# The down projection of a streaming-encoder layer, recast from eight block products to seven

## The chip, the cores and the metric

The kernel runs on one core of a Trainium2 chip. The metric is the device time of one execution in microseconds (us), lower is better. The kernel before the change takes 1774.91 us (median of 3 runs, 1773.05 to 1775.65).

## What is computed

One layer of a hybrid encoder over 1056 rows (1024 of a prompt and 32 of a decoded sample), model width 1024. It has a mixing block (differential attention and retention) that ends in an addition to `h`, then a feed-forward block, then a gated addition. The part that matters here is the feed-forward block and what follows it:

```
f = rmsnorm(h, g_ffn)
g = f @ w_g;  u = f @ w_u                  # 1024 -> 2816
s = gelu(causal_dwconv3(g) + conv_b) * u
h = h + s @ w_d                            # 2816 -> 1024
h = h + (pe @ w_pe) * sigmoid(rmsnorm(h, g_pe) @ w_pg)
```

Everything is float32 in and out.

## The kernel before

Activations are held with features on the partitions and the 1056 rows along the free axis. A float32 product is made as three TensorE matmuls in a float32 format of reduced precision: each operand is split into a high part (a ScalarE copy) and a low part (a VectorE subtraction, `split_x` lines 251 to 258 and `split_w` lines 210 to 223), and `mm3` (line 242) issues high x high, high x low and low x high into one PSUM tile.

The instructions are written with a tile framework. It takes the order of the program as a priority, and each engine's queue is laid out ahead of time by a scheduler which may put a later instruction first where it reckons the earlier one not ready. An engine then works its queue strictly in that order. Buffers come from pools: a tag with `bufs=n` has n slots, and a new tile waits for a slot. Where a pool is opened on the bytes of a closed pool, its tiles wait for every user of the closed one. Nearly all loads, and the stores to the scratch tensors of this stage, are issued by SyncE's queue through `load` (line 110).

Up phase (lines 1265 to 1294). A loop over 11 blocks `b` of 256 columns makes `g` and `u` for two 128-feature tiles at a time. Each of the two products is done with seven block products instead of eight (`strassen`, line 1204, the form with fifteen additions): the rows are cut in two halves of HT = 528, the contraction in two halves, the columns in two halves of 128. Matmuls there have 264 columns (SC = HT/2). GpSimd makes the sums of weights (lines 1194 to 1200). VectorE then runs the convolution, ScalarE the gelu, GpSimd multiplies `g` by `u` (line 1293), and each finished 128 x 1056 tile of `s` goes to the scratch tensor `d_s` (line 1294). The tiles of this phase (`lx`, `ly`, `snap`, `wraw1`) lie in a pool named `late`; its `ly` tiles have six slots. The operands of the seven products lie partly in tag `A` of the pool `act` (16 slots), partly in `late`.

Down phase (lines 1323 to 1344). The 22 tiles of `s` are taken in groups of 2, 4, 4, 4, 4 and 4. A group is loaded from `d_s`, split, and multiplied by the matching rows of `w_d`, in four units `u` of 256 output columns; each unit has two 128-feature tiles `m` and three chunks of 352 rows (`fm`, line 261, PSUM tag `g` with three slots). Line 1342 adds each PSUM chunk to `hT[m]`, which is loaded from `d_h` in the first group. In the last group, `fin(m)` squares `hT[m]` (lines 969 to 975, the sum of squares on GpSimd for most m) and splits `hT[m]` times a gain for the last projection (lines 257 and 258).

End (from line 1347). `rms_rows` turns the sum of squares into a row factor `rb2`; then `w_pg` is applied to all of `f2`, eight tiles deep, and line 1358 multiplies each PSUM chunk by `rb2`.

## Time and profile before

| | |
|---|---|
| median of 3 runs | 1774.91 us |
| the profiled execution | 1772.96 us, of which the span is 1771.2 us |
| PE busy | 1747.2 us (99%) |
| VectorE (DVE) busy | 1085.8 us (61%) |
| ScalarE (ACT) busy | 722.3 us (41%) |
| GpSimd (POOL) busy | 329.7 us (19%) |
| up phase, roughly | 950 to 1403 us of the span |
| down phase, roughly | 1399 to 1662 us |

PE is TensorE's matmul stream, PEld its weight loads, SP is SyncE (SPq its queue of transfers). Matmuls are pipelined, so the duration of one is longer than the distance from one to the next; how many fall in a stretch is the better measure. `L1342` is line 1342 of the kernel. `out<-in` names what an instruction writes and reads.

### The profile page before, as it was taken

Reading aid. Unit: us, or ns where it says so; the run is one execution under the profiler, and the core shown is the slowest. Engines: PE = TensorE matmul, PEld = TensorE weight load, DVE = VectorE, ACT = ScalarE, POOL = GpSimd, SP = SyncE. Lnnn points to the kernel's source line nnn. Section 1 sums busy time; section 2 is a strip of 40 time slices with the busy share of each in tenths; the row PEclk is TensorE's granted clock in tenths of the full one; section 3 lists DMA queues with packets and bytes.
Section 4 is the critical chain, followed back from the end, with each engine's and each line's share of the span. In section 5 each row is a group of like instructions: output and inputs, shape, how many; then the busy total and the mean of one; then the engine's idle time right before and its main releaser. Section 6 shows DMA issues by size and latency. Waiting matters only on the chain.

```text
span 1771.2 us, 31680 instructions
## 1 busy us (share of the span) xinstructions
PE 1747.2 (99%) x12626; PEld 1719.7 (97%) x12626; DVE 1085.8 (61%) x2352; ACT 722.3 (41%) x1623; POOL 329.7 (19%) x356
## 2 busy tenths in 40 slices
PE   7999999999999999999999999999999999999998
PEld 7998999999999999999999999999999999999998
DVE  7766766666664564565468866665566664444644
ACT  6536664656423433322346433443333421112332
POOL 6110001000121021000002433344443200001111
PEclk9999999999999999999999999999999999999999
DMA  9311222222222214544443222222222552211331
GB/s 289 107 49 41 72 73 76 83 67 78 71 79 65 74 63 142 205 146 138 159 161 125 85 83 86 73 73 73 73 85 90 203 208 97 73 38 47 110 110 50
DMA packets 136858, 178.12 MB, mean 101 GB/s; under 512 B 9645, under 2 KB 115973, under 8 KB 136709
## 3 DMA queue, kind: packets, MB, share of 16 engines
q1 hardware_dynamic: 119976, 145.53, 25.5%
q0 software_dynamic: 8896, 26.06, 4.2%
q10 hardware_dynamic: 7837, 4.51, 0.9%
q8 instruction: 99, 1.62, 0.4%
q14 instruction: 50, 0.41, 0.1%
HBM read 128.92 MB, written 47.14 MB: 99 GB/s over the span
## 4 chain that ended last, share of the span: by engine, by line
PE 91%; DVE 4%; DMA 3%; ACT 1%; issue 1%; SPq 0%; ACTq 0%; DVEq 0%
PE gt L247 19%; PE gt L248 19%; PE gt L249 19%; PE gt L1220 4%; PE gt L1221 4%; PE gt L1219 4%; PE st L1220 2%; PE st L1221 2%; PE st L1219 2%; PE mt L659 2%; PE mt L1219 1%; PE mt L1220 1%; PE mt L1221 1%; PE st L622 1%; PE st L623 1%; PE gt L478 1%
## 5 line engine op out<-in xcount | busy, mean ns | idle before, releaser
L247 PE MATMUL gt<-apair,whi 128*128 128x352 f32 x672 | 219.5, 327 | 0.1
L248 PE MATMUL gt<-apair,whi 128*128 128x352 f32 x672 | 219.1, 326 | 0.0
L249 PE MATMUL gt<-apair,wlo 128*128 128x352 f32 x672 | 218.4, 326 | 0.0
L1179 DVE TENSOR_TENSOR wlo<-wraw,whi 128x512 fp32r<-128x512 f32 x154 | 140.2, 918 | 102.7 <-ACT whi L1178 101.8
L220 ACT ACTIVATE whi<-wraw 128x512 fp32r<-128x512 f32 x196 | 119.2, 629 | 203.0 <-PE gt L248 174.4
L247 PE MATMUL gt<-sA,whi 128*128 128x352 f32 x528 | 170.3, 323 | 1.3 <-DVE lx L1342 1.3
L248 PE MATMUL gt<-sA,whi 128*128 128x352 f32 x528 | 170.3, 322 | 0.0
L249 PE MATMUL gt<-sA,wlo 128*128 128x352 f32 x528 | 170.3, 322 | 0.0
L1178 ACT ACTIVATE whi<-wraw 128x512 fp32r<-128x512 f32 x154 | 96.8, 632 | 171.8 <-PE st L1220 69.0
L221 DVE TENSOR_TENSOR wlo<-wraw,whi 128x512 fp32r<-128x512 f32 x196 | 135.2, 706 | 27.9 <-ACT whi L220 25.0
L1221 PE MATMUL gt<-opt,wlo 128*128 128x264 f32 x528 | 150.5, 285 | 1.2 <-DVE wlo L1179 1.2
L1220 PE MATMUL gt<-opt,whi 128*128 128x264 f32 x528 | 150.4, 285 | 0.0
L1219 PE MATMUL gt<-opt,whi 128*128 128x264 f32 x528 | 149.8, 284 | 0.5 <-ACT whi L1178 0.5
L247 PE MATMUL gt<-whi,apair 128*128 128x256 f32 x512 | 147.4, 289 | 0.4 <-DVE apair L378 0.4
L248 PE MATMUL gt<-wlo,apair 128*128 128x256 f32 x512 | 146.9, 287 | 0.0
L249 PE MATMUL gt<-whi,apair 128*128 128x256 f32 x512 | 146.3, 286 | 0.0
L1342 DVE TENSOR_TENSOR lx<-lx,gt 128x352 f32<-128x352 f32 x144 | 73.6, 517 | 92.6 <-PE gt L249 92.5
L249 PEld LDWEIGHTS gt<-apair,wlo 128*128 128x128 f32 x672 | 126.3, 188 | 1.9 <-issue 0.2
L247 PEld LDWEIGHTS gt<-apair,whi 128*128 128x128 f32 x672 | 126.4, 188 | 1.7 <-DVE etile L781 0.3
L248 PEld LDWEIGHTS gt<-apair,whi 128*128 128x128 f32 x672 | 126.5, 188 | 1.4
L247 PEld LDWEIGHTS gt<-sA,whi 128*128 128x128 f32 x528 | 99.1, 188 | 2.0 <-DVE lx L1342 1.9
L1221 PEld LDWEIGHTS gt<-opt,wlo 128*128 128x128 f32 x528 | 99.2, 188 | 1.4 <-DVE wlo L1179 1.4
(419 smaller groups left out, 4991.0 us busy)
## 6 DMA issues: line engine op xcount, KB each, us to landing
wraw<-in_w_in SPq DMA_DIRECT2D x28, 512.0 KB, 4.0
d_s<-ly SPq DMA_DIRECT2D x22, 528.0 KB, 2.7
wraw<-in_w_g SPq DMA_DIRECT2D x22, 512.0 KB, 5.1
wraw<-in_w_u SPq DMA_DIRECT2D x22, 512.0 KB, 3.8
wraw<-in_w_d SPq DMA_DIRECT2D x20, 512.0 KB, 3.6
d_gt<-etile POOLq DMA_DIRECT2D x48, 176.0 KB, 2.1
ly<-d_gt SPq DMA_DIRECT2D x16, 528.0 KB, 3.7
ly<-d_s SPq DMA_DIRECT2D x16, 528.0 KB, 4.7
```

The source lines that it names most:

```text
L220: S.activation(hi, r, AF.Copy)
L221: V.tensor_tensor(out=lo, in0=r, in1=hi.bitcast(F32), op=ALU.subtract)
L247: PE.matmul(ps, wh, xh, start=first and i == 0, stop=False)
L248: PE.matmul(ps, wh, xl, start=False, stop=False)
L249: PE.matmul(ps, wl, xh, start=False, stop=last and i == n - 1)
L659: PE.matmul(po, pt[:, i * 128:i * 128 + 128], v[:, b + i, :], start=b + i == 0, stop=b + i == t)
L1178: S.activation(h3, src, AF.Copy)
L1179: V.tensor_tensor(out=l3, in0=src, in1=h3.bitcast(F32), op=ALU.subtract)
L1219: PE.matmul(ps, wh[:, ws], xh, start=start and k == 0, stop=False, skip_group_check=True)
L1220: PE.matmul(ps, wh[:, ws], xl, start=False, stop=False, skip_group_check=True)
L1221: PE.matmul(ps, wl[:, ws], xh, start=False, stop=k == n - 1, skip_group_check=True)
L1342: V.tensor_tensor(out=hT[m][:, c0:c0 + n], in0=hT[m][:, c0:c0 + n], in1=ps, op=ALU.add)
```

## The change

The down projection is recast in the same seven-product form. The contraction of 2816 is cut in two halves by the parity of the 128-feature tile (j = 0 or 1, 11 tiles each), the rows in two halves of 528, and each unit of 256 output columns in two halves of 128. For each of the seven products in turn, over all four units, 11 tiles deep, two chunks of 264 rows are accumulated in PSUM and then added to the halves of `hT` that need them. The seven row operands (four quarters and their sums) are made by VectorE at the end of each block of the up phase and go to a new scratch tensor `d_q` instead of `d_s` (NB = 11 below). Sums of weights are made by GpSimd. The pool `late` is closed after the up phase, and a pool `down` is opened on its bytes, with a pool `sums` inside that is closed ahead of the seventh product and replaced by a pool `last`.

```
+    d_q = dram.tile([7 * NB * 128, HT], F32, name="d_q")
...
+    lps = ctx.enter_context(ExitStack())
+    lp = pool("late", stack=lps)
...
+    QROWS = ("b11", "t2", "b21", "b22", "t3", "t1", "t4")
...
                 G.tensor_tensor(out=ss[j][:, a:e], in0=ss[j][:, a:e], in1=ys[j][:, a + o:e + o], op=ALU.mult)
-            load(d_s[ft * 128:(ft + 1) * 128, :], ss[j])
+        (b11_, b12_), (b21_, b22_), (t3_, t1_) = ((x[:, 0:HT], x[:, HT:T]) for x in (ss[0], ss[1], ys[0]))
+        t4_ = ys[1][:, 0:HT]
+        V.tensor_tensor(out=t3_, in0=b22_, in1=b12_, op=ALU.subtract)
+        V.tensor_tensor(out=t1_, in0=b11_, in1=b12_, op=ALU.subtract)
+        V.tensor_tensor(out=b12_, in0=t3_, in1=b11_, op=ALU.add)
+        V.tensor_tensor(out=t4_, in0=b12_, in1=b21_, op=ALU.subtract)
+        for n, x in ((0, ss[0]), (2, ss[1]), (4, ys[0])):
+            load(q_rows(n, 2, b), x[:, 0:T].rearrange("p (n c) -> p n c", n=2))
+        load(q_rows(6, 1, b), t4_.unsqueeze(1))
...
+    lps.close()
+    PRODUCTS = ("b21", "b11", "t1", "t2", "t3", "b22", "t4")
+    dn = pool("down")
+    hT = [dn.tile([128, T], F32, name="hT", tag="H", bufs=KD) for _ in range(KD)]
+    for m in range(KD):
+        load(hT[m], d_h[m * 128:(m + 1) * 128, :])
...
+    def stage(n, b):
+        nm = PRODUCTS[n]
+        q = QROWS.index(nm)
+        if n == 0:
+            if b % 2 == 0:
+                c = min(2, NB - b)
+                staged = ap_.tile([128, 2, HT], F32, name="stg", tag="A", bufs=16)
+                load(staged[:, 0:c, :], q_rows(q, 1, b, c))
...
+            return
+        raw = dn.tile([128, HT], F32, name="stg", tag="T", bufs=3)
+        load(raw, q_rows(q, 1, b)[:, 0, :])
+        split_row(n, b, raw)
...
+    def raw_w(i, j, u, own=None, wide=None):
+        src = wv[j][:, :, u * 256 + i * 128:u * 256 + i * 128 + 128]
+        nraw[0] += 1
+        if wide is None:
+            wide = nraw[0] % 2
+        if own is None and not wide:
+            ta, tb = (wp.tile([128, 1024], F32, name="wraw", tag="raw", bufs=2) for _ in range(2))
+            load(ta.rearrange("p (k c) -> p k c", c=128), src[:, 0:8, :])
+            load(tb[:, 0:384].rearrange("p (k c) -> p k c", c=128), src[:, 8:NB, :])
+            return [ta[:, 0:512], ta[:, 512:1024], tb[:, 0:384]]
+        t = own if own is not None else dn.tile([128, NB * 128], F32, name="wr", tag="W", bufs=1)
+        load(t.rearrange("p (k c) -> p k c", c=128), src)
+        return [t[:, 0:512], t[:, 512:1024], t[:, 1024:1408]]
...
+        elif nm == "t1":
+            t = sb.tile([128, NB * 128], F32, name="wsum", tag="B", bufs=4)
+            w = wsum[u] = add_w(raw_w(1, 0, u, own=t), raw_w(1, 1, u, wide=u % 2))
+        elif nm == "t2":
+            w = add_w(wsum[u], raw_w(0, 0, u))
+        elif nm == "b22":
+            w = add_w(wsum[u], raw_w(0, 1, u))
+        else:
+            w = add_w(raw_w(0, 0, u, wide=u % 2), raw_w(1, 0, u, wide=1 - u % 2))
...
+    for n, nm in enumerate(PRODUCTS):
+        if n == 6:
+            sbs.close()
+            lp, ybufs = pool("last"), 5
         for u in range(4):
...
+            ws = product_w(n, u)
+            he, ho = hT[2 * u], hT[2 * u + 1]
+            for c0 in (0, SC):
+                ps = gt(SC)
+                mm3(ps, ws, [(xo[n, k][:, 0, c0:c0 + SC], xo[n, k][:, 1, c0:c0 + SC]) for k in range(NB)])
+                a, b_ = slice(c0, c0 + SC), slice(HT + c0, HT + c0 + SC)
+                if nm == "b21":
+                    acc_into(he[:, a], ps)
+                elif nm == "b11":
+                    copy(rr[u][:, a], ps)
+                    acc_into(he[:, a], ps)
+                elif nm == "t1":
+                    acc_into(he[:, b_], ps)
+                    acc_into(ho[:, b_], ps, ALU.subtract)
+                elif nm in ("t2", "t3"):
+                    acc_into(rr[u][:, a], ps)
+                elif nm == "b22":
+                    acc_into(he[:, b_], ps)
+                else:
+                    acc_into(ho[:, a], ps, ALU.subtract)
+            if nm == "t2":
+                acc_into(he[:, HT:T], rr[u])
+            elif nm == "t3":
+                acc_into(ho[:, HT:T], rr[u], ALU.subtract)
+                acc_into(ho[:, 0:HT], rr[u], ALU.subtract)
+            if n < 6:
+                for b in range(3 * u, min(3 * u + 3, NB)):
+                    stage(n + 1, b)
+            else:
+                for m in ((0, 2), (4, 6), (1, 3), (5, 7))[u] if u < 3 else ():
                     fin(m)
+    fin(5)
+    fin(7)
```

`split_row` splits a staged row operand into a tile of tag `A`, or of a new tag `Q` (six slots in `down`) for the first six tiles of every second product. `acc_into` is one VectorE addition or subtraction, `add_w` three GpSimd additions (128 x 512, 512 and 384). `rr` holds running sums in 128 x 528 pieces.

## Rows read from the trace of the kernel before

**Rows 1.** The page: span and busy time of each engine, and the chain that ended last, by engine.

```profile
span 1771.2 us, 31680 instructions
...
PE 1747.2 (99%) x12626; PEld 1719.7 (97%) x12626; DVE 1085.8 (61%) x2352; ACT 722.3 (41%) x1623; POOL 329.7 (19%) x356
...
PE 91%; DVE 4%; DMA 3%; ACT 1%; issue 1%; SPq 0%; ACTq 0%; DVEq 0%
```

**Rows 2.** Windows of the span: start:end and length, then busy time (and instructions) of PE, PEld, DVE, ACT and POOL, granted TensorE clock, DMA share and GB/s. Two windows of the up phase, the change of phase, two windows of the down phase.

```profile
1100.00:1200.00 100.00, 100.00 (x822) 100.00 (x821) 63.03 (x111) 40.88 (x80) 37.73 (x30) 1.00 0.23 75
1200.00:1300.00 100.00, 100.00 (x823) 100.00 (x822) 58.30 (x105) 38.40 (x77) 42.26 (x31) 1.00 0.27 86
...
1400.00:1450.00 50.00, 48.71 (x313) 48.00 (x312) 34.59 (x57) 14.35 (x21) 6.68 (x6) 1.00 0.83 304
1450.00:1500.00 50.00, 50.00 (x315) 50.00 (x314) 23.36 (x40) 10.11 (x14) 0.00 (x0) 1.00 0.26 86
1500.00:1550.00 50.00, 50.00 (x314) 50.00 (x313) 23.39 (x40) 8.85 (x12) 0.00 (x0) 1.00 0.24 75
```

**Rows 3.** What PE waited for from 1380 us to the end: us in total, times, longest.

```profile
PE gt L247 <- DVE lx L1342: 1.3, 2, 1.0
PE mt L1370 <- ACT mtile L134: 0.8, 1, 0.8
```

**Rows 4.** Instructions by line and shape, 1410 to 1650 us (the down phase): busy us, mean ns of one, idle before.

```profile
L1342 DVE TENSOR_TENSOR lx<-lx,gt 128x352 f32<-128x352 f32 x135 | 69.1, 518 | 92.6 <-PE gt L249 92.5
L221 DVE TENSOR_TENSOR wlo<-wraw,whi 128x512 fp32r<-128x512 f32 x44 | 31.5, 721 | 12.9 <-ACT whi L220 12.9
L220 ACT ACTIVATE whi<-wraw 128x512 fp32r<-128x512 f32 x44 | 27.5, 629 | 139.8 <-PE gt L248 119.4 <-DMA wraw<-in_w_d 13.7 <-issue 5.1
L255 DVE TENSOR_TENSOR sA<-ly,sA 128x1056 fp32r<-128x1056 f32 x16 | 19.9, 1251 | 2.8 <-ACT sA L254 2.8
...
L975 POOL TENSOR_TENSOR ly<-ly 128x1056 f32<-128x1056 f32 x4 | 9.9, 2470 | 227.8 <-ACT ly L974 227.8
```

**Rows 5.** The same for 1100 to 1300 us (the up phase): the multiplication on GpSimd, one of its additions of weights, an addition from PSUM.

```profile
L1293 POOL TENSOR_TENSOR ly<-ly 128x1024 f32<-128x1024 f32 x10 | 24.9, 2512 | 7.3 <-ACT ly L1257 7.3
...
L1194 POOL TENSOR_TENSOR wraw<-wraw,wraw 128x512 f32<-128x512 f32 x10 | 12.9, 1286 | 114.9 <-DVE wlo L1179 114.9
L1262 DVE TENSOR_TENSOR ly<-mt,snap 128x264 f32<-128x264 f32 x20 | 8.1, 422 | 0.0
```

**Rows 6.** Transfers. From the page: SyncE's queue over the whole span (packets, MB, share of 16 engines), the store of a tile of `s` and a load of weights (KB each, median us to landing). From the window 381 to 388 us, in which nearly all packets of the queue are of 512 bytes: the queue. From the window 1405 to 1425 us: GB/s in 40 slices, and the queue.

```profile
q1 hardware_dynamic: 119976, 145.53, 25.5%
...
d_s<-ly SPq DMA_DIRECT2D x22, 528.0 KB, 2.7
...
wraw<-in_w_d SPq DMA_DIRECT2D x20, 512.0 KB, 3.6
...
q1 hardware_dynamic: 1080, 0.54, 26.7%
...
GB/s 359 291 259 358 374 389 414 422 422 397 378 383 384 410 417 412 422 414 406 438 414 406 397 422 414 422 366 385 355 387 367 442 418 406 414 422 397 389 367 379
...
q1 hardware_dynamic: 3354, 7.82, 102.3%
```

**Rows 7.** The earlier change of pools, from `p1` to `late`: what SyncE's queue waited for from 690 to 701 us; the last VectorE instruction that reads a tile of `p1` (`ft`); the first loads into `late` (start, us).

```profile
SPq L110 <- DVE mtile L867: 13.8, 1, 13.8
...
699.10 0.25 DVE L867 SCALAR_TENSOR_TENSOR mtile<-mt,gda,ft 128x32 f32<-128x32 f32 x1 [1.73 <-PE mt L865]
...
699.50 0.81 SPq L110 DMA_DIRECT2D ly<-d_od  x2
```

**Rows 8.** The end of the up phase in order of time (start us, us): two VectorE instructions, three multiplications on GpSimd, and the loads of `hT`.

```profile
1398.15 1.82 SPq L110 DMA_DIRECT2D lx<-d_h  x4
...
1405.21 5.40 POOL L1293 TENSOR_TENSOR ly<-ly 128x1024 f32<-128x1024 f32 x3 [2.39 <-ACT ly L1257]
...
1407.00 0.49 DVE L1262 TENSOR_TENSOR ly<-st,snap 128x232 f32<-128x232 f32 x2 [3.29 <-PE st L1221]
...
1408.29 2.22 DVE L221 TENSOR_TENSOR wlo<-wraw,whi 128x512 fp32r<-128x512 f32 x1 [0.36 <-ACT whi L220]
```

**Rows 9.** The end of the down phase in order of time: one addition of squares on GpSimd, the split of `hT` beside it and one without company, the last addition from PSUM, and the two instructions by which `rb2` reaches the first chunk of the last projection.

```profile
1640.08 2.46 POOL L975 TENSOR_TENSOR ly<-ly 128x1056 f32<-128x1056 f32 x1 [3.84 <-ACT ly L974]
...
1641.03 2.62 DVE L258 SCALAR_TENSOR_TENSOR f<-lx,cvec,f 128x1056 fp32r<-128x1056 f32 x1 [1.00 <-ACT f L257]
...
1659.88 1.31 DVE L258 SCALAR_TENSOR_TENSOR f<-lx,cvec,f 128x1056 fp32r<-128x1056 f32 x1
...
1662.47 0.52 DVE L1342 TENSOR_TENSOR lx<-lx,gt 128x352 f32<-128x352 f32 x1
...
1675.08 0.69 DVE L1000 COPY ly<-mt 128x512 f32<-128x512 f32 x1 [4.21 <-PE mt L995]
1675.80 0.52 DVE L1358 TENSOR_TENSOR etile<-gt,ly 128x352 f32<-128x352 f32 x1
```

**Rows 10.** The first 30 us in three windows, columns as in rows 2.

```profile
0.00:10.00 10.00, 3.02 (x10) 1.90 (x10) 4.07 (x26) 5.30 (x11) 2.83 (x9) 1.00 0.82 244
10.00:20.00 10.00, 7.04 (x41) 6.65 (x41) 6.84 (x18) 2.77 (x8) 3.60 (x5) 1.00 1.03 367
20.00:30.00 10.00, 9.67 (x67) 9.28 (x67) 9.40 (x41) 8.43 (x21) 8.31 (x13) 0.83 1.07 317
```

More of the change, by code (lines that the diff above doesn't have):

```diff
@@ L908, in layer_kernel @@
         gate_unit(6)
-    lp = pool("late")
+    lps = ctx.enter_context(ExitStack())
+    lp = pool("late", stack=lps)
+    ybufs = 6
     def xtile(dt=F32):
@@ L916, in ytile @@
     def ytile(n=T, dt=F32):
-        return lp.tile([128, n], dt, name="ly", tag="Y", bufs=6, padded_shape=[128, 1060])
+        return lp.tile([128, n], dt, name="ly", tag="Y", bufs=ybufs, padded_shape=[128, 1060])
     def snap():
@@ L1301, in layer_kernel @@
     store(O["conv_sample"].rearrange("o b w (f p) -> (o b w f) p", p=128), ct[44:88, 0:128])
-    hT = [None] * KD
-    f2 = []
+    lps.close()
[4 more added lines that the diff above has]
+        load(hT[m], d_h[m * 128:(m + 1) * 128, :])
+    r2 = (rstd_b, dn.tile([128, T], F32, name="r2", tag="R", bufs=1))
+    rr = [r2[u // 2][:, u % 2 * HT:u % 2 * HT + HT] for u in range(4)]
+    sbs = ctx.enter_context(ExitStack())
+    sb = pool("sums", stack=sbs)
+    wsum = [None] * 4
+    wv = I["w_d"][0].rearrange("(b j p) c -> j p b c", j=2, p=128)
+    f2 = [None] * KD
     acc2 = [None]
@@ L1310, in f2_tile @@
         nx[0] += 1
[L1311 to L1312 removed]
+        if nx[0] <= 6:
+            return dn.tile([128, T], F32R, name="f2q", tag="Q", bufs=6)
+        if nx[0] == 7:
+            return dn.tile([128, T], F32R, name="f2r", tag="R", bufs=1)
         return ap_.tile([128, T], F32R, name="f2", tag="A", bufs=16)
@@ L1320, in fin @@
             split_x(fp[0][:, cs], fp[1][:, cs], hT[m][:, cs], gpe[:, m:m + 1])
[L1321 to L1343 removed]
+        f2[m] = fp
@@ new lines, in split_row @@
+    def split_row(n, b, raw):
+        if n % 2 and b < 6:
+            t = dn.tile([128, 2, HT], F32R, name="oq", tag="Q", bufs=6)
+        else:
+            t = ap_.tile([128, 2, HT], F32R, name="oq", tag="A", bufs=16)
+        split_x(t[:, 0, :], t[:, 1, :], raw, -1.0 if PRODUCTS[n] == "t2" else None)
+        xo[n, b] = t
+    nraw = [1]
+    def raw_w(i, j, u, own=None, wide=None):
[11 more added lines that the diff above has]
+        return [t[:, 0:512], t[:, 512:1024], t[:, 1024:1408]]
@@ new lines, in add_w, with product_w @@
+    def add_w(dst, src):
+        for x, y in zip(dst, src):
+            G.tensor_tensor(out=x, in0=x, in1=y, op=ALU.add)
+        return dst
+    def product_w(n, u):
+        nm = PRODUCTS[n]
+        if nm == "b21":
+            w = raw_w(0, 1, u)
+        elif nm == "b11":
+            w = raw_w(0, 0, u)
+        elif nm == "t4":
+            w = raw_w(1, 1, u)
+        elif nm == "t1":
[7 more added lines that the diff above has]
+            w = add_w(raw_w(0, 0, u, wide=u % 2), raw_w(1, 0, u, wide=1 - u % 2))
+        parts = []
+        for x in w:
+            c = x.shape[1]
+            hi = wp.tile([128, 512], F32R, name="whi", tag="hi", bufs=6)
+            lo = wp.tile([128, 512], F32R, name="wlo", tag="lo", bufs=6)
+            split_x(hi[:, :c], lo[:, :c], x)
+            parts.append((hi, lo))
+        return [tuple(y[:, k % 4 * 128:k % 4 * 128 + 128] for y in parts[k // 4]) for k in range(NB)]
@@ new lines, in acc_into @@
+    def acc_into(dst, src, op=ALU.add):
+        V.tensor_tensor(out=dst, in0=dst, in1=src, op=op)
+    for b in range(NB):
+        stage(0, b)
+    for b in range(NB):
+        split_row(0, b, xo.pop(("raw", b)))
+    for n, nm in enumerate(PRODUCTS):
+        if n == 6:
+            sbs.close()
+            lp, ybufs = pool("last"), 5
+        for u in range(4):
+            ws = product_w(n, u)
[4 more added lines that the diff above has]
+                a, b_ = slice(c0, c0 + SC), slice(HT + c0, HT + c0 + SC)
+                if nm == "b21":
+                    acc_into(he[:, a], ps)
+                elif nm == "b11":
+                    copy(rr[u][:, a], ps)
[17 more added lines that the diff above has]
+                    stage(n + 1, b)
+            else:
+                for m in ((0, 2), (4, 6), (1, 3), (5, 7))[u] if u < 3 else ():
```

30 lines of the change are left out of this document (6 added, 24 removed).

## The prediction

> **What bounds the kernel now.** I read the page first: PE is busy 99% of the span and carries 91% of the chain that ended last [rows 1]. Then the windows: in the up phase and in the down phase PE is busy every microsecond at full clock, while DVE, ACT, POOL and the DMA engines have room; only the change between the two phases shows a gap, 1.3 us of 50 [rows 2]. Then the waits of PE: 1.3 us for VectorE at that change and 0.8 us later, nothing else [rows 3]. So the stage pays for matmuls by number and width, and whatever the change adds costs time only where it makes PE wait. The work is to count matmuls, then to look for places where the new form leaves PE without operands, weights or PSUM.
>
> **Term 1, the matmuls.** Before: 22 tiles x 8 m x 3 chunks x 3 passes = 1584 matmuls of 352 columns. 315 and 314 of them fall in two windows of 50 us [rows 2], so one takes 0.1590 us and all take 251.8 us. After: 7 products x 4 units x 2 chunks x 11 tiles x 3 passes = 1848 of 264 columns. The up phase issues just these, 822 and 823 in 100 us [rows 2]: 0.1216 us each, 224.7 us. An eighth less arithmetic therefore gives back only 10.8% of the time, since the narrower matmul costs more per column: **-27.1 us**. A unit (66 matmuls) lasts 8.03 us, a chunk 4.01.
>
> **Term 2, the change of phase.** All tiles of `down` wait for every user of `late`. The earlier change of pools shows it: SyncE sat 13.8 us, and its first loads left 0.15 us after the last reader of an old tile had ended [rows 7]. There PE had other units to run; here little is left. Call the end of the last up matmul T0.
> - What can run: the first product's row operands lie in `act`, outside the closed pool, and its rows (b21) come from `ss[1]`, stored early; the weights of unit 0 use the old `raw` slots, and after them those of unit 2. Unit 1's weights go to tag `W` in `down`. With three PSUM slots and no `hT` to add into, PE can run unit 0 and half of unit 2, to T0 + 12.
> - When the pool opens: the last additions from PSUM (0.8 us after the matmul, as 1407.00 + 0.49 [rows 8]), the product of `g` and `u` for one tile on POOL (2.51 us, and 0.5 for its 32 last columns [rows 5]), the four new VectorE instructions of 528 elements (half of 1251 ns [rows 4], some 0.65 us each, 2.6), then the last stores: 2.7 us for one alone [rows 6], and some 1.2 us more since three are under way, 1.35 MB in all. T0 + 10.3.
> - What then stands in SyncE's queue, by program order: eight loads of `hT` (4.33 MB, 11 us at the 390 GB/s of the saturated queue [rows 6]), three row tiles of the second product (0.8 MB, 2.1 us), and only then unit 1's weights: 1408 packets of 512 bytes. The window with such packets alone gives 0.267 x 7 us x 16 / 1080 = 27.7 ns each [rows 6], so 2.4 us over 16 engines. With some 2 us from issue to first bytes (3.6 us of landing for a load that needs 1.4 us) and 1.6 us of splitting (0.63 on ACT, 0.7 on DVE [rows 4], 0.3 between them): T0 + 29.4.
> - `hT[0]` lands at T0 + 13.7, which frees PSUM for the other half of unit 2. PE thus has 16.06 us of work in 29.4: it stands some 13.3 us, less the 1.3 us of today [rows 2]: **+12**. That the scheduler puts unit 2 ahead of unit 1 I take from the loads of `hT` that today run 4 to 9 us ahead of the last up-phase work on POOL and DVE [rows 8]: the queues don't keep program order where something is late. Bounds: 3.4 (weights ahead of `hT`) and 20.1 (no reordering), both worked out under the rivals.
>
> **Term 3, the clock.** After ten microseconds with PE busy 3.02 and ten with 7.04, the granted clock of the next ten was 0.83 although PE was busy 9.67 of them [rows 10]: 1.7 us at full speed were lost. The gap of term 2 is of that kind; today's 1.3 us left the clock at 1.00 [rows 2]. **+1.7**, bounds 0 and 3.4 (two such falls).
>
> **Term 4, the up phase.** Each block (41 us) gets four VectorE instructions, 2.6 us, on an engine that is 58 to 63% busy there, and four transfers for two, on DMA engines 0.23 to 0.27 busy [rows 2]. The cover is PE's own queue of matmuls; six `ly` slots still meet six tiles a block, held some 4 us longer, and the next block needs its third to sixth tile only half a block later. **+1**; bounds 0 and 29 (11 x 2.6, every instruction on the path), the value being near the end that today's gapless windows suggest.
>
> **Term 5, inside the seven products.** What DVE needs per unit: three splits of weights (0.69 + 0.69 + 0.53 = 1.9), 2.75 splits of row tiles (1.8), two additions from PSUM at 0.42 [rows 4, 5], two more in `t1`, one addition of 528 (0.65) in `t2`, two in `t3`. So 4.6 us in `b21`, `b11`, `b22` and `t4` (ahead of `fin`), 5.4 in `t1`, 5.2 in `t2`, 5.9 in `t3`, out of 8.03. POOL adds weights in four products: 1.29 + 1.29 + 0.97 = 3.55 us a unit [rows 5]. But the two don't run freely side by side: a weight split that takes 0.72 us took 2.22 beside the multiplications of POOL, and ended with them, at 1410.5 [rows 8]; a split of `hT` took 2.62 us beside POOL and 1.31 alone [rows 9]. An addition from PSUM kept its 0.52 us throughout [rows 4, 9]. So I add POOL's time to that of the DVE instructions with two SBUF inputs: `t1` 7.25, `t2` 7.9, `t3` 8.55, `b22` 7.25, and count half of the PSUM additions behind them: 8.1, 8.3, 9.0, 7.7 us, four units each, 132 against PE's 128.5. Weights are split up to two units ahead (six slots, three a unit) and the light second product gives room, so part of the 3.8 us is absorbed: **+2**, bounds 0 and 12. Transfers: in `t3` a unit moves 2816 packets (4.9 us) and 0.8 MB of rows (2.0), 6.9 of 8.03; its weight loop (4.5 us to land, 3.6 adding, 1.3 splitting, 9.4) is longer than a unit, but over four units it falls behind by 4 us of the 8 it leads.
>
> The Trainium skill, "SBUF — State Buffer", section "Who interferes with whom", says that a VectorE instruction with two SBUF inputs and a GpSimd instruction that reads SBUF share an exclusive port, the later one waiting for the whole of the other. The rows above agree for VectorE; that POOL waits as well no row shows. It speaks against this change, and becomes the first rival.
>
> **Term 6, the tail.** The eight `fin` had four units of 11.4 us; now they have 32 us. In SBUF instructions: 8 splits at 1.31, weights 4 x 1.9 and 2.8 for `w_pg`, five additions of squares on POOL at 2.47 and 2.8 us on DVE [rows 4, 9] make 36 us against PE's 32.1. Half of these can start early, since even m are complete one product before. Today `rb2` is in use 13.3 us after the last addition from PSUM [rows 9] and PE just covers it (three chunks of 24 matmuls, 11.5 us, and the transposes), so lateness counts in full: **+3**, bounds -1 and +8.
>
> **The sum.** -27.1 + 12 + 1.7 + 1 + 2 + 3 = -7.4 us on an execution of 1772.96 (span 1771.2 and 1.76 around it): 1765.6. The median of the runs lies 1.95 us above that execution: **1767.5 us**, 0.4% faster. A change of this kernel can be told from none by about 0.2%, 3.5 us.
>
> **The rivals.**
> - *The shared port of DVE and POOL sets the pace of `t1` to `b22` and of `fin`.* If PSUM additions don't fit beside POOL, a unit takes 8.94, 8.75, 9.4 and 8.1 us: 12.3 us over PE, and the tail 8. It decides once a unit's sum exceeds 8.03 us for more units than the two of lead. -27.1 + 12 + 1.7 + 1 + 12.3 + 8 = +7.9: 1782.8, slower. For it: instructions that ended with POOL's. Against: today's up phase has both engines busy and no wait of PE [rows 2]. 0.17.
> - *PE keeps the written order of units.* It stands from T0 + 8.03 to 29.4, 21.4 us, less 1.3: term 2 is 20.1, and the result 1775.6, no change. Against: [rows 8]. 0.16.
> - *Unit 1's weights go ahead of `hT`.* They land at T0 + 14.7, `hT[0]` at 16.1; its addition frees PSUM at 16.7, so PE stands 4.7 us after its 12.0 of work, term 2 is 3.4, and the fall of the clock costs 0.8 less: 1758.1. For it: SyncE's queue is laid out by need, too. 0.20.
> - *Small packets throttle the stage.* 50,688 of 512 bytes at 60 ns, the mean over all packets of this queue (0.255 x 1771.2 us x 16 / 119976 [rows 6]), would be 190 us of all 16 engines, and 20.8 MB of rows 53 more: 243 against 224.7, +18 over the terms less the gap: about 1783. Against: the 27.7 ns of packets of this size. 0.05.
> - The forecast: 0.42.
>
> **How the numbers follow.** Faster by over 0.2% (below 1771.4): four fifths of the forecast, all of the third rival, a fifth of the second: 0.57. Within 0.2%: the rest of the forecast, most of the second rival, a little of the first: 0.19. Slower: 0.24. The range 1754 to 1784 reaches from the third rival, with terms 5 and 6 at their low ends, to the first with its full price; the forecast's own range is 1760 to 1776.
>
> **What would show it.** 1848 matmuls of 264 columns at 0.1216 us; a gap of 10 to 16 us in PE within 30 us of the last up matmul, ended by a split of weights loaded to tag `W`, and a granted clock below 1.00 in that stretch; SyncE waiting for the last user of `late`; in `t3`, PE waiting for weights or PSUM for under 5 us; PE waiting for `rb2` by about 3 us at the start of the last projection. Wrong would be: no gap at the change of phase, waits of over 10 us spread over `t1` to `b22`, or a gap in the up phase.

## The result and the profile after

The kernel after takes 1796.48 us (median, 1794.56 to 1800.66) where the kernel before takes 1774.07 beside it: a ratio of 1.0129, 95% interval 1.0106 to 1.0151. It is 1.3% slower; the prediction was 1767.5 us, and its range ended at 1784.

The page of the kernel after, the lines that answer to [rows 1]:

```profile
span 1796.5 us, 32815 instructions
...
PE 1733.9 (97%) x12890; PEld 1703.5 (95%) x12890; DVE 1144.1 (64%) x2423; ACT 767.0 (43%) x1726; POOL 399.6 (22%) x404
...
PE 10%; DMA 5%; DVE 2%; POOL 1%; SPq 1%; issue 1%; ACT 1%; DVEq 0%; POOLq 0%; ACTq 0%
```

PE is busy 13 us less, yet the span is 25.3 us longer. The chain that ended last now carries transfers, VectorE and GpSimd beside PE (its shares add up to some 21% because it reaches back only to 1415.7 us, where the down phase begins): the stage is no longer bound by matmuls alone. The windows (columns as in [rows 2]) show where:

```profile
1100.00:1200.00 100.00, 100.00 (x822) 100.00 (x821) 67.31 (x121) 40.63 (x79) 37.55 (x29) 1.00 0.28 92
...
1410.00:1420.00 10.00, 7.35 (x46) 7.35 (x47) 9.35 (x15) 1.62 (x3) 0.62 (x2) 0.67 0.54 186
1420.00:1430.00 10.00, 2.44 (x21) 2.23 (x19) 0.80 (x3) 0.00 (x0) 0.00 (x0) 0.84 1.00 398
1430.00:1440.00 10.00, 2.99 (x13) 2.99 (x14) 4.96 (x9) 4.73 (x9) 0.00 (x0) 0.50 1.06 319
...
1500.00:1550.00 50.00, 43.28 (x336) 43.07 (x336) 32.20 (x44) 14.03 (x26) 26.95 (x19) 0.93 0.61 173
1550.00:1600.00 50.00, 47.43 (x383) 46.60 (x382) 34.66 (x54) 20.06 (x34) 9.65 (x7) 1.00 0.61 179
1600.00:1650.00 50.00, 42.46 (x315) 41.63 (x316) 35.78 (x44) 20.53 (x34) 24.65 (x17) 0.93 0.48 137
```

The up phase is as gapless as before. At the change of phase PE does 12.8 us of work in 30, and at a lower clock; then it loses again and again, most where POOL is busy. What PE waited for, from 1395 to 1690 us in three stretches (us in total, times, longest):

```profile
PE gt L248 <- ACT whi L255: 14.6, 1, 14.6
PE gt L249 <- DVE oq L256: 5.6, 1, 5.6
...
PE gt L248 <- DVE hT L1432: 8.5, 2, 6.7
...
PE gt L250 <- DVE wlo L256: 2.7, 2, 2.1
PE gt L248 <- DVE rstd_b L1432: 2.4, 2, 1.3
```

(`whi` and `wlo` are split weights, `oq` split rows, `hT` and `rstd_b` additions that free PSUM.) One measure serves all that follows: the **loss** of a unit is the distance from its first matmul to that of the next unit, less 8.03 us. Undisturbed units last 8.03 to 8.06 us, as predicted. The loss of the 28 units is 52.6 us: 41.6 in 15 gaps of over 0.3 us, 10.5 in 106 matmuls at half clock (0.22 us apart for 0.12), the rest small (the profiled execution took 1798.3 us, 1.8 above the median). By product, in the order in which they run, in us: b21 24.0, b11 3.8, t1 9.4, t2 3.0, t3 3.1, b22 9.3, t4 0.0. The last up matmul starts within 0.2 us of where it did before, so the account is: from it to the last addition of the phase 277.9 us, where before it was 255.8 (1662.47 [rows 9] less 1406.68), +22.1; behind that +3.4.

**The two waits at the change of phase**, in order of time (start us, us): VectorE, then SyncE's queue, then the two splits of weights on ACT.

```profile
1410.65 0.71 DVE L1308 TENSOR_TENSOR ly<-ly 128x528 f32<-128x528 f32 x1 [3.31 <-POOL ly L1304]
...
1411.90 1.32 DVE L256 TENSOR_TENSOR oq<-stg,oq 128x528 fp32r<-128x528 f32 x2
...
1412.01 4.67 SPq L111 DMA_DIRECT2D d_q<-ly  x3
1418.64 4.04 SPq L111 DMA_DIRECT2D hT<-d_h  x8
1422.73 2.51 SPq L111 DMA_DIRECT2D stg<-d_q  x3
1426.22 0.38 SPq L111 DMA_DIRECT2D wr<-in_w_d  x1
...
1436.33 1.56 ACT L255 ACTIVATE whi<-wr 128x512 fp32r<-128x512 f32 x3 [2.14 <-DMA wr<-in_w_d]
1437.80 1.55 ACT L255 ACTIVATE whi<-wraw 128x512 fp32r<-128x512 f32 x3
```

The 5.6 us lie inside unit 0: the low splits of its row tiles stand on VectorE behind the last block's row sums, and the first of these waits for POOL's multiplication. The 14.6 us follow the predicted order: the pool opens 12.1 us after the last up matmul (1406.5), `hT` goes first, the rows of b11, then unit 1's weights into tag `W`, split from 1436.3 on. But on ACT the weights of unit 2 (`wraw`, loaded into old slots before) are split behind them, as written, so PE could run no matmul of unit 2 in between.

**One of the later waits**, the 6.7 us that end at 1513.64, in the same columns:

```profile
1500.91 4.73 POOL L1402 TENSOR_TENSOR wsum<-wsum,wraw 128x512 f32<-128x512 f32 x3
...
1504.38 1.66 SPq L111 DMA_DIRECT2D wraw<-in_w_d  x2
1506.09 1.43 SPq L111 DMA_DIRECT2D stg<-d_q  x3
...
1511.86 0.64 ACT L258 ACTIVATE oq<-stg 128x528 fp32r<-128x528 f32 x1 [10.34 <-DMA stg<-d_q]
...
1512.53 0.71 DVE L259 SCALAR_TENSOR_TENSOR oq<-stg,oq 128x528 fp32r<-128x528 f32 x1 [7.76 <-ACT oq L258]
1513.16 0.42 DVE L1432 TENSOR_TENSOR hT<-hT,gt 128x264 f32<-128x264 f32 x1
```

Read it from the end. PE's next chunk needs the PSUM slot that the addition at 1513.16 frees. Its operand was there when PE's wait began, but it stands on VectorE behind a row split; the split waits for ACT, ACT for a row tile's load; the load stands on SyncE behind two weight loads, and these wait for slots that POOL's additions of weights free. Five queues, each in order, none of them full.

### The profile page after: what moved, and what is told of

It is laid out like the page before. It is cut to its first block, busy times and chain, and to the rows that moved or that the text cites. A ratio compares the mean times of both kernels' runs of the same rounds, so it can differ in the third digit from the quotient of the medians.

```text
span 1796.5 us, 32815 instructions
## 1 busy us (share of the span) xinstructions
PE 1733.9 (97%) x12890; PEld 1703.5 (95%) x12890; DVE 1144.1 (64%) x2423; ACT 767.0 (43%) x1726; POOL 399.6 (22%) x404
## 5 line engine op out<-in xcount | busy, mean ns | idle before, releaser
L248 PE MATMUL gt<-oq,whi 128*128 128x264 f32 x616 | 180.2, 293 | 30.4 <-ACT whi L255 16.2
L1183 DVE TENSOR_TENSOR wlo<-wraw,whi 128x512 fp32r<-128x512 f32 x154 | 140.0, 917 | 82.5 <-ACT whi L1182 81.5
L249 PE MATMUL gt<-oq,whi 128*128 128x264 f32 x616 | 180.2, 293 | 5.6 <-DVE oq L256 5.6
L250 PE MATMUL gt<-oq,wlo 128*128 128x264 f32 x616 | 180.1, 293 | 2.8 <-DVE wlo L256 2.7
L1182 ACT ACTIVATE whi<-wraw 128x512 fp32r<-128x512 f32 x154 | 96.8, 632 | 171.8 <-PE st L1224 68.0
L248 PEld LDWEIGHTS gt<-oq,whi 128*128 128x128 f32 x616 | 121.0, 197 | 32.2 <-ACT whi L255 18.0
L249 PEld LDWEIGHTS gt<-oq,whi 128*128 128x128 f32 x616 | 120.7, 196 | 5.8 <-DVE oq L256 5.8
L250 PEld LDWEIGHTS gt<-oq,wlo 128*128 128x128 f32 x616 | 120.8, 196 | 3.4 <-DVE wlo L256 3.4
L221 ACT ACTIVATE whi<-wraw 128x512 fp32r<-128x512 f32 x152 | 91.8, 629 | 63.9 <-PE gt L249 56.8
L222 DVE TENSOR_TENSOR wlo<-wraw,whi 128x512 fp32r<-128x512 f32 x152 | 103.9, 702 | 15.8 <-ACT whi L221 12.2
```

Source lines behind the costliest of these rows:

```text
L221: S.activation(hi, r, AF.Copy)
L222: V.tensor_tensor(out=lo, in0=r, in1=hi.bitcast(F32), op=ALU.subtract)
L248: PE.matmul(ps, wh, xh, start=first and i == 0, stop=False)
L249: PE.matmul(ps, wh, xl, start=False, stop=False)
L250: PE.matmul(ps, wl, xh, start=False, stop=last and i == n - 1)
L1182: S.activation(h3, src, AF.Copy)
```

## The experiments

Losses in us, by the measure above. The kernel before took 1773.4 to 1774.1 beside them throughout. e1 to e10 are one execution each, and the four of the kernel after lie between 1794.6 and 1800.7, so times a few us apart are not told apart by one execution; the losses come from one profiled execution. In e1, e4, e7, e8 and e11 to e15 the first matmul of the phase starts 1.36 us after the last up matmul, for 0.12 in the kernel after; these 1.24 us the table leaves out.

```
kernel                 median us   b21   b11  t1 to t4
after                    1796.48  24.0   3.8   24.8
e1_first_weights         1789.43  17.8   6.3   19.8
e4_first_psum            1789.88  17.1   6.4   21.5
e2_no_weight_sums        1785.43  24.2   2.3   13.9
e9_sums_on_dve           1786.67  24.7   5.4   12.8
e5_rows_no_load          1790.38  26.5   0.0   18.5
e6_rows_act_queue        1788.26  25.7   1.7   16.8
e10_no_sums_no_loads     1771.72  27.5   0.0    0.0
e3_rows_once             1766.21  22.2   0.0    0.0
e8_sums_later            1784.31  12.1   3.9   22.3
e7_change_of_phase       1783.97   8.6   3.7   26.8
e11_ordered              1783.26   7.3  11.7   21.3
e12_ordered_dve          1778.18   7.1  19.9    9.2
e13_two_queues           1770.15  14.2   2.2    9.4
e14_less_at_once         1767.31   8.5   5.2    8.4
e15_splits_first         1765.76   5.6   4.0   10.2
```

Against the expectations below: e8, e9, e10 and e13 came out as one of their theories had it, to within a microsecond. e2 and e5 came out as their rivals had it, with 14 and 18 us still lost from t1 on, and e3 lost nothing there. Outside what any of their theories had put lie e1 (7 us gained, for 15 to 19 or under 6), e6 (16.8 us left, for under 12) and e12 (9.2 us left, for under 8, and 1778 us for 1757 to 1768). e4 stayed with e1 instead of falling to 1774 to 1779, and e7 and e11 lost 12.3 and 19.0 us in the first two products where under 7 and 8 were expected, as their rivals had it. e14 and e15 are taken up at their place.

### The gap: e1 and e4

e1 loads all weights of the first product into the old slots, which are open early.

```
-            w = raw_w(0, 1, u)
+            w = raw_w(0, 1, u, wide=0)
```

> The changed kernel, with all four units of the first product loading their weights into the old raw slots, none into the tag W of the pool that opens late. Theory A (the gap of 14.6 us after unit 0 is unit 1's weights, which stand behind the close of the old pool and eight loads of hT, while PE keeps the written order): the gap shrinks to the wait for hT[0], under 4 us, and the clock falls once less, so 15 to 19 us less than the changed kernel's 1796. Rival (hT itself is what is late; weights are only the last to arrive): the gap stays over 10 us, ended by an addition into hT, and the time changes by less than 6 us. Neither expects a change in the waits of the later products, some 20 us.

The 14.6 us went, but the time fell by 7 only. The waits of PE from 1395 to 1490 us:

```profile
PE gt L249 <- DVE oq L256: 5.1, 1, 5.1
PE gt L248 <- ACT whi L255: 3.7, 1, 3.7
PE gt L248 <- issue: 2.8, 1, 2.8
PE gt L248 <- ACT oq L255: 1.7, 2, 1.1
PE gt L248 <- DVE hT L1432: 1.7, 1, 1.7
```

The wait for rows stayed (5.1); the one of 14.6 has become five shorter ones: on weights, on rows, on PSUM and, in one ("issue"), on nothing that the profile names. e4 adds more PSUM slots for the first product:

```
-                ps = gt(SC)
+                ps = (gt, gt, st, st, mt, mt, gt, st)[2 * u + (c0 > 0)](SC) if n == 0 else gt(SC)
```

> The edit of e1, and the first product's eight chunks in PSUM tiles of all three tags, so that no matmul of it waits for an addition into hT. Theory A: only the wait for the last block's row tile (5.6 us at 1412 in the changed kernel) is left of the 20 us, 1774 to 1779; if hT paces e1, e4 is faster than e1 by what e1's gap still shows, otherwise the two are within 2 us.

No gain: PSUM waiting for `hT` isn't what limits that stretch.

### From b11 on: sums of weights, row loads, or both (e2, e9, e5, e6, e10, e3)

e2 leaves the additions of weights out and keeps their loads.

```
-        for x, y in zip(dst, src):
-            G.tensor_tensor(out=x, in0=x, in1=y, op=ALU.add)
         return dst
```

> The changed kernel with GpSimd's additions of weights left out: the products t1, t2, t3 and b22 multiply by one of their loaded weights instead of the sum; all loads stay. Theory B (the additions pace the weight slots, SyncE's in-order queue waits there with the row loads behind, and the PSUM additions wait behind the row splits): the excess of 24 us in the units of t1 to b22 over 8.03 us each falls below 6 us, time 1772 to 1780. Rival B1 (the row tiles, by their loads and splits alone, are late whatever POOL does): at least 12 us of the excess stay, time above 1784. Both leave the 20 us at the change of phase.

e9 makes the same sums on VectorE.

```
-            G.tensor_tensor(out=x, in0=x, in1=y, op=ALU.add)
+            V.tensor_tensor(out=x, in0=x, in1=y, op=ALU.add)
```

> The changed kernel with the 48 additions of weights on VectorE in place of GpSimd. Theory D (in t1 to b22 the additions on POOL and the row and weight splits on DVE hold each other up at a shared port, so each unit pays POOL's 3.55 us on DVE's side; on DVE the same additions take some 1.9 us and nothing waits for a port): the excess of 24 us after the first product falls to 8 to 18 us, what late row loads alone leave (16 us in e2), time 1782 to 1791. Rival D1 (DVE is simply full, port or not): 1.9 us more a unit on DVE makes it worse, above 1798.

e5 leaves the row loads out from b11 on: one tile that stays in place is split each time.

```
-        load(raw, q_rows(q, 1, b)[:, 0, :])
-        split_row(n, b, raw)
+        split_row(n, b, ident_row)
```

> The changed kernel with the 66 later row tiles split as before, but all from one tile that is loaded once: the loads of row tiles are left out, the splits on ACT and DVE and all weights and sums stay. Theory C (row loads arrive late, because they stand in SyncE's in-order queue behind weight loads that wait for a slot, and PSUM additions stand on DVE behind the splits of the late rows): the waits after the first product vanish to under 4 us, as they did in e3, and the time is 1765 to 1771. Rival C1 (the engine time of the splits beside POOL, the shared port): 10 us or more of the 24 us stay, 1776 or above.

e6 keeps the loads, and issues them from ScalarE's queue.

```
-        load(raw, q_rows(q, 1, b)[:, 0, :])
+        S.dma_start(out=raw, in_=q_rows(q, 1, b)[:, 0, :])
```

> The changed kernel with the 66 later loads of row tiles issued by ScalarE's queue instead of SyncE's. Theory C: rows no longer stand behind weight loads, so the excess of 24 us in the later products falls below 12 us, time 1779 to 1787. If the transfers themselves are the limit (bytes and packets), nothing changes: 1793 to 1799. If ScalarE's queue takes over the blocking, since it waits for a row slot that DVE frees, waits for splits of weights grow and the time may exceed 1796.

e10 has the edits of e2 and e5 together; e3 takes the first product's row operands for all seven, with neither loads nor splits of rows, and keeps the sums.

```
-                    stage(n + 1, b)
+                    xo[n + 1, b] = xo[0, b]
```

> The edits of e2 and e5 together: no additions of weights and no loads of the 66 later row tiles; all splits and all weight loads stay. Theory E (two separate causes, the additions beside the splits and the late row loads; the splits alone fit): no wait is left after the first product, as in e3, time 1766 to 1771 (with the gap of the change of phase at 18 to 23 us). Rival E1 (the splits alone overfill DVE or ACT): 5 us or more stay, above 1773.

> The changed kernel with the row operands of the first product used for all seven: the 66 later row tiles are neither loaded nor split; the additions of weights stay. Theory B (the weight loop and POOL are too slow, rows only pass the delay on to the PSUM additions): with no row split ahead of a PSUM addition most waits for hT go, but waits for weights in t1, t3 and b22 stay: 4 to 12 us of the 24 us remain, time 1775 to 1788. Rival B1 (rows alone): all of it goes and the later products run without a wait, time near 1771. Rival B2 (the port shared by VectorE and POOL sets the pace): DVE loses 1.8 us a unit, and the waits for weights go as well.

Four of these make a square. Loss from b11 to t4: both 28.6, no sums 16.2, no row loads 18.5, neither 0.0. Either cause alone costs 16 to 18 us, taking only one away gives back 10 to 12, and without both the splits, the additions from PSUM and 1848 matmuls fit exactly. e6 gives as much as having no row loads at all (18.5): what hurt was their place in SyncE's queue behind weight loads, not their bytes. e9 gives nearly as much as having no sums (18.2 against 16.2), though VectorE then does more: what hurt was their being on POOL beside VectorE, not the sums. The instructions by line and shape, 1450 to 1690 us (busy us, mean ns of one, idle before), in the kernel after:

```profile
L256 DVE TENSOR_TENSOR oq<-stg,oq 128x528 fp32r<-128x528 f32 x50 | 40.2, 827 | 36.7 <-ACT oq L255 36.5
L256 DVE TENSOR_TENSOR wlo<-wsum,whi 128x512 fp32r<-128x512 f32 x24 | 25.6, 1092 | 3.7 <-ACT whi L255 3.7
...
L1402 POOL TENSOR_TENSOR wsum<-wsum,wr 128x512 f32<-128x512 f32 x12 | 17.8, 1502 | 10.2 <-DMA wr<-in_w_d 7.4 <-DVE wlo L256 2.7
```

and in e9:

```profile
L256 DVE TENSOR_TENSOR oq<-stg,oq 128x528 fp32r<-128x528 f32 x50 | 34.3, 706 | 21.4 <-ACT oq L255 21.2
L256 DVE TENSOR_TENSOR wlo<-wsum,whi 128x512 fp32r<-128x512 f32 x24 | 16.0, 685 | 0.2 <-ACT whi L255 0.2
...
L1402 DVE TENSOR_TENSOR wsum<-wsum,wr 128x512 f32<-128x512 f32 x12 | 7.8, 687 | 10.7 <-DMA wr<-in_w_d 10.7
```

A weight split takes 1092 ns beside POOL and 685 without; POOL's addition takes 1502 ns here and 1286 in the up phase [rows 5]. Both engines lose. VectorE does the same addition in 687 ns, in less than half of POOL's time, so e9 alone doesn't separate a slow POOL from the two engines holding each other up.

e3 helps to separate them: it is without row work and loses nothing from b11 on, although its sums are still on POOL and hardly faster there, as its row for the same instruction shows.

```profile
L1402 POOL TENSOR_TENSOR wsum<-wsum,wr 128x512 f32<-128x512 f32 x12 | 16.9, 1429 | 8.5 <-DMA wr<-in_w_d 8.5
```

POOL's own pace is therefore enough, and e5, which differs from e3 by the row splits alone, loses 18.5 us. That fits a VectorE which, with the row splits gone, has room for the stretched rest.

### The change of phase: e8, e7, e11, e12

e8 is e1 with t1's own weight loads, 2.9 MB that stood in the first 40 us, held behind b11's last row load (`after` fixes an order of two instructions).

```
-        load(t.rearrange("p (k c) -> p k c", c=128), src)
+        ld = nc.sync.dma_start(out=t.rearrange("p (k c) -> p k c", c=128), in_=src)
+        if own is not None:
+            after(ld, rows_last[1])
```

> The edit of e1 and one more: the four loads of t1's own weight tiles (2.9 MB), which SyncE's queue issues right after the pool opens, are held back until the last row tile of the second product has been issued. Theory A2 (after e1 the change of phase is bound by what stands in the transfer queue ahead of the second product's rows): the 24 us that units 0.0 to 1.3 of e1 lost fall to 10 to 17 us, time 1779 to 1785. Rival (hT alone, 4.3 MB, fills that time): less than 3 us gained on e1's 1789.

e7 adds that only the four quarters of `hT` that b21 needs are loaded first, the others behind b11's rows, and that the last block's row sums are written behind the first product's splits.

```
-    for m in range(KD):
-        load(hT[m], d_h[m * 128:(m + 1) * 128, :])
+    for m in range(0, KD, 2):
+        load(hT[m][:, 0:HT], d_h[m * 128:(m + 1) * 128, 0:HT])
```

> The edits of e8 and two more: only the four hT halves that the first product adds into are loaded at first, the other twelve after the second product's rows; and in the last block the four VectorE sums stand behind the splits of the first product's rows. Theory A (the change of phase is loads in the wrong order, and the 5.6 us wait at its start is the row splits standing behind VectorE instructions that wait for POOL): units 0.0 to 1.3 lose under 7 us in place of 28, the later products still their 20 or so, time 1768 to 1776. Rival (the stores and the close of the old pool set the gap whatever the order): over 12 us stay lost there, above 1780.

b21 lost 3.5 us less than in e8, and what was put off seems to have returned in t1, which lost 10.8 us for 5.4; its rows stood behind the loads that were put off. e11 puts each load behind the weights of the product before instead, sends all row loads through ScalarE's queue, gives chunks 4 to 6 other PSUM slots and orders the first of the four row sums behind the low splits; e12 is e11 with the sums of weights on VectorE.

```
+            if early:
+                after(first, before_sums)
...
+                ps = st(SC) if n == 0 and 3 <= 2 * u + (c0 > 0) < 6 else gt(SC)
```

> The changed kernel with its order mended: the first product's weights all in the old slots; its six chunks 0 to 5 in two PSUM tags; the last block's VectorE sums behind the splits of the first product's rows; four halves of hT first, the other twelve and t1's own weight tiles each behind a weight load of the product before; row tiles on ScalarE's queue. Additions of weights stay on GpSimd. Theories A, C and D: units 0.0 to 1.3 lose under 8 us in place of 28, the later ones 12 to 18 us as in e5 and e6: 1766 to 1776. If the change of phase is bound by the stores and the pool whatever the order: above 1780.

> e11 with the additions of weights on VectorE. Theory D: the later products lose under 8 us, 1757 to 1768, faster than the kernel before. Rival D1 (DVE full): slower than e11 by 5 us or more.

Both were slower than before: ratios 1.0042 (1.0025 to 1.0059) and 1.0027 (1.0017 to 1.0036). b21 now lost 7 us, and b11, the product behind it, 12 and 20 (in profiled executions that lie 3.6 and 3.8 us above their medians). Windows of e12, columns as in [rows 2]:

```profile
1425.00:1445.00 20.00, 20.00 (x167) 20.00 (x166) 9.66 (x18) 7.42 (x13) 0.00 (x0) 1.00 0.98 309
1445.00:1465.00 20.00, 15.16 (x105) 14.32 (x104) 8.04 (x14) 5.85 (x10) 0.00 (x0) 0.91 1.11 323
1465.00:1485.00 20.00, 12.29 (x81) 11.98 (x80) 9.53 (x19) 7.07 (x14) 0.00 (x0) 0.67 0.65 192
```

and SyncE's queue from 1425 to 1465 us (packets, MB, share of 16 engines):

```profile
q1 hardware_dynamic: 13964, 9.14, 79.6%
```

For 40 us the DMA engines were full (the rest of the share is ScalarE's queue), at 309 and 323 GB/s, where [rows 6] shows some 400: a packet of SyncE's queue has 0.65 KB here and 2.3 KB there. I read e7 to e12 so that whatever is asked for last in that stretch comes late, and an order only chooses which product waits; e14 puts that to the test.

### Both causes mended: e13 to e15

The expectations below describe two edits wrongly: in e13 it is the third product's (t1's) weights that are held behind the second's last row load, and only the second product's rows stay on SyncE; in e14 the last four quarters of `hT` stand behind t1's weights.

e13 is e8 with the edit of e9 and this one:

```
-        rows_last[n] = nc.sync.dma_start(out=raw, in_=q_rows(q, 1, b)[:, 0, :])
+        rows_last[n] = (nc.sync if n == 1 else S).dma_start(out=raw, in_=q_rows(q, 1, b)[:, 0, :])
```

> As e8 (the first product's weights through the older raw slots, the second product's weight loads behind the last row load of the third), with the sums of weights on VectorE, and with the row loads of the fourth and later products on ScalarE's queue; those of the second and third stay on SP. The arithmetic is that of the kernel after. Theory order (what is lost at the change of phase is transfers standing in the wrong order in their queues): the change of phase loses about what e8 lost there, 16 us over undisturbed units, and the products behind it 8 to 12 us as in e12, so 1766 to 1773 us. Theory saturation (the transfer engines are full for the first 60 us of the phase whatever the order): 16 us at the change of phase too, since the same bytes are moved in it; this run is the one that e14 is set against.

e14 moves loads out of the first 60 us (its edit as set against e13):

```
+            for m, h in {1: ((2 * u, HT), (2 * u + 1, HT)), 3: ((2 * u + 1, 0),)}.get(n, ()):
+                after(nc.sync.dma_start(out=hT[m][:, h:h + HT], in_=d_h[m * 128:(m + 1) * 128, h:h + HT]),
+                      rows_last[1] if n == 1 else w_last[2, 3])
...
-            after(ld, rows_last[1])
+            after(ld, w_last[2, u - 1] if u else rows_last[1])
```

> e13 with some 5 MB of loads moved out of the first 60 us of the down phase: of the sixteen halves of hT only the four that the first output chunks need are read at first, eight behind the rows of the second product, the other four behind the second product's own weights; each weight block is read for the sums one unit ahead and no earlier. Theory saturation: the first two products lose under 8 us over undisturbed units, where e13 loses about 16, and the time is 1760 to 1768 us. Theory order: the same loss at the change of phase as in e13, within 3 us, and the time of e13.

e13 took 1770.15 us, ratio 0.9983 (0.9974 to 0.9992), and e14 1767.31, ratio 0.9964 (0.9950 to 0.9977). In b21 and b11 they lost 16.4 and 13.7 us. So neither theory came out as it was put: e14 didn't fall below 8, and 2.7 us is within the 3 that the theory of order allowed. By units it is clearer. Both lose 7.8 us in the very first unit, where PE waits for splits of rows that were loaded early; behind it e13 loses 8.6 and e14 5.9. The windows of e13, and then of e14, show the relief in the first stretch and the load returning in the last:

```profile
1420.00:1440.00 20.00, 17.57 (x145) 17.36 (x143) 5.50 (x11) 2.99 (x5) 0.00 (x0) 1.00 1.00 357
...
1470.00:1490.00 20.00, 18.83 (x154) 18.54 (x152) 16.67 (x31) 10.91 (x22) 0.00 (x0) 1.00 0.93 266
```

```profile
1420.00:1440.00 20.00, 20.00 (x167) 20.00 (x166) 9.66 (x18) 7.02 (x13) 0.00 (x0) 1.00 0.80 234
...
1470.00:1490.00 20.00, 18.96 (x155) 18.75 (x155) 14.16 (x26) 8.37 (x17) 0.00 (x0) 1.00 1.06 296
```

e15 is aimed at the 7.8 us: all four row sums of the last block behind the low splits, with the PSUM slots of e11.

```
+                add = V.tensor_tensor(out=o, in0=x, in1=y, op=op)
+                if early:
+                    after(add, before_sums)
```

> As e14, with all four row sums of the last block, on VectorE, ordered behind the low splits of the first product's row tiles (e11 had moved one of the four), and the fourth to sixth output chunk in other PSUM tags, since hT then arrives later. Theory queue: what is left at the start of the down phase, 7.9 us in the first unit, comes from the low splits standing in VectorE's queue behind a row sum that waits for GpSimd's multiplication; then the wait of 5.1 us falls to under 2 us, the first unit loses under 4 us, and the time is 1761 to 1765 us. Theory splits: the ten splits themselves and the last tile's way through the scratch tensor take that long; then the wait stays at 4 to 5 us and the time at that of e14, 1767 us, or above it, since the loads of the second product leave later.

1765.76 us, ratio 0.9949 (0.9935 to 0.9963): of all kernels here that compute the whole layer the fastest, 0.5% under the kernel before. The first unit lost 5.6 us, between the two theories. PE's waits from 1395 to 1500 us, what VectorE and POOL did, and the durations of the ten low splits (ns, least, median, longest):

```profile
PE gt L249 <- DVE oq L256: 5.4, 3, 3.3
PE gt L248 <- ACT oq L255: 3.0, 2, 2.0
...
1409.40 8.47 DVE L256 TENSOR_TENSOR oq<-stg,oq 128x528 fp32r<-128x528 f32 x10
...
1406.46 5.90 POOL L1304 TENSOR_TENSOR ly<-ly 128x1024 f32<-128x1024 f32 x3 [3.18 <-ACT ly L1268]
...
L256 DVE TENSOR_TENSOR oq<-stg,oq x10: 694/696/2854, 1409.4 to 1417.2; 128x528 fp32r<-128x528 f32 x10
```

The splits no longer stand behind a sum that waits for POOL, but the first of them runs beside POOL's multiplication: it takes 2.85 us, where the others take 0.7, and ends within 0.1 us of it, at 1412.3. PE's longest wait there, 3.3 us, ends with this split. So the place in the queue was worth some 2 us, and most of the rest is again POOL beside VectorE, which neither theory had.

What e15 still loses, some 20 us over the phase, isn't settled in full. In t3 (4.2 us) VectorE isn't full, since it is busy 26.5 of 36.3 us. The longest wait there, 2.2 us, ends with this addition from PSUM:

```profile
1584.02 0.69 DVE L1402 TENSOR_TENSOR wsum<-wsum,wr 128x512 f32<-128x512 f32 x1 [3.05 <-DMA wr<-in_w_d]
...
1586.30 0.42 DVE L1432 TENSOR_TENSOR r<-r,gt 128x264 f32<-128x264 f32 x1
```

It stands behind sums of weights for whose load VectorE itself had been idle for 3 us: on VectorE a sum that waits for its weights holds up the additions that free PSUM.

## Why the prediction was wrong, term by term

- **Term 1 (matmuls, -27.1): right.** Undisturbed units last 8.03 us. All of the loss lies outside this term.
- **Term 2 (change of phase, +12): wrong in two steps.** The pool opened at 12.1 us after the last up matmul (10.3 predicted) and PE resumed at 30.5 (29.4). The step that failed is that PE would run unit 2 before unit 1: it kept the written order and stood 20.2 us (5.6 and 14.6), in size the second rival's 21.4. But that rival, too, let unit 0 run through; that its rows were ready because they are stored early is the other step that failed: PE stood 5.6 us inside unit 0. Here that added little, since unit 1's weights were later still; in e1 it shows, with 5.1. The loads of `hT` in [rows 8] show a load that was put ahead, not a matmul. The trace of the kernel before does show that: PE ran 11 matmuls of the down phase between the last chunks of the up phase, here the last of them,

```profile
1405.18 0.32 PE L248 MATMUL gt<-sA,whi 128*128 128x352 f32 x1
1405.34 0.28 PE L1219 MATMUL st<-opb,whi 128*128 128x264 f32 x1
```

  so the premise wasn't groundless. Why the splits of unit 2's weights, and with them its matmuls, were left in the written order this time, no run shows. e1 shows that this step alone was worth 7 us, not all of the gap: behind the late weights stood full transfer engines (e12) and late splits of rows (e15). The term's 27.7 ns for a packet of 512 bytes came from a load by itself; with the engines full a packet of 0.65 KB took 36 ns (0.796 x 40 us x 16 / 13964).
- **Term 3 (clock, +1.7): too small.** I counted one fall. There were seven stretches of half clock from 1409 to 1697 us, behind the waits of the single products as well; matmuls at half clock cost 10.5 us and the start of the tail 1.8. The longer waits were thus paid for a second time.
- **Term 4 (up phase, +1): right.** PE's first up matmul lay 1.05 us later than before (938.75 for 937.70 us), and from 979 to 1395 us every one 1.61 us later, so the phase lost 0.6 at most. That the last one lies where it did is chance: the 11 matmuls of the down phase that ran ahead of it before, 1.7 us, are no longer there.
- **Term 5 (inside the products, +2, at most 12): mis-sized, the largest error.** It measured 28.6 us, clock falls among them. POOL beside VectorE, which I took in as the first rival at 12.3 us, was worth 10 to 12 (e9, e2). The size is that rival's, the mechanism only in part: it had VectorE overfull, and VectorE was busy 32 to 36 us of each 50 from 1500 to 1650 us; the stretched instructions cost time by what stood behind them. Nor did it decide alone, since without it e9 is still slower than before. The other cause I didn't have: transfers were counted by volume, 6.9 us of 8.03 in t3, and volume did fit, but not their order. The row loads stand in one queue with weight loads that wait for slots (e6: 10 us).
- **Term 6 (tail, +3): the size right, the reason not.** It measured +3.4:

```profile
1684.42 0.42 DVE L1432 TENSOR_TENSOR hT<-hT,gt 128x264 f32<-128x264 f32 x1
...
1684.00:1700.00 16.00, 16.00 (x100) 15.97 (x99) 5.99 (x21) 2.48 (x5) 0.00 (x0) 0.89 0.59 202
```

  From 1684.4 to the end there are 112.1 us, for 108.7 from 1662.47 [rows 9]. But PE didn't wait for `rb2` by 3 us; it was busy all 16 us, at a clock of 0.89, which costs 1.8 of them. The last 1.6 us I can't place.

The sum of the terms as measured: -27.0 for matmuls, +52.6 of losses, less the 4.0 us by which the phase was longer than its 1584 matmuls before (255.8 less 251.8), +3.4: 25.0 of the 25.3 us between the spans. The fourth rival, small packets, was given 0.05 and 1783 us (by its own terms, +18 and less the gap's 12, it would be 1773.5). As a price over the whole stage it falls: with every load in place the engines were 0.48 to 0.61 busy from 1500 to 1650 us, and a packet took 36 ns where they were full, not 60. For the first 60 us it holds in so far as the engines were full there.

The prediction cited the Trainium skill, "SBUF — State Buffer", section "Who interferes with whom", for an exclusive port between VectorE and GpSimd, and left open whether GpSimd waits as well. It does: 1502 ns for 1286 (one of its additions, in t1 to b22 and in the up phase).

## What to carry to other kernels

Going from eight products to seven gives back what the matmuls say, to a tenth of a microsecond, only while PE never waits; work that was one deep loop over operands in place becomes seven passes that reload, split and sum, so count for each queue what stands ahead of what, not only how full it is. Where a stage is near one engine's pace, take loads with different partners apart into different queues, keep elementwise work off GpSimd while VectorE is at work on SBUF operands, and spread loads that crowd the start of a stage: together (e15) these turned +1.3% into -0.5%. And don't let a forecast rest on a reordering by the scheduler: that it put matmuls ahead in one kernel did not mean that it would in the next.

## What was not expected of the hardware

- GpSimd loses to VectorE as VectorE does to it: three additions of weights took 4.73 us at 1500.91 and 3.44 with VectorE idle at 1505.94.
- Two causes of waiting don't add: 16.2 and 18.5 us alone, 28.6 together.
- Full DMA engines moved 398 GB/s while `hT` came in (1420 to 1430 us) and 319 in the next 10 us, with weights in 512-byte packets, at shares of 1.00 and 1.06.
